# Seven-product feed-forward of a two-layer decoder trunk: the last product of each group moved behind the first of the next, and the matmuls of a product ordered bank by bank

## The chip, the cores and the metric

The kernel runs on one core of one Trainium2 chip. The metric is the device time of one execution in microseconds (us). The engines are called by their short names: PE is the matrix engine (PEld its weight loads), DVE the vector engine, ACT the scalar engine, POOL the general one, and SP the queue that issues nearly all DMA transfers. PSUM is the memory of 8 banks into which PE accumulates; SBUF holds everything else.

## The reference, cut to what matters

Two layers; each is a half-step SwiGLU feed-forward, a mixing block of three attentions, and a second half-step SwiGLU, with RMSNorm around each. Only the feed-forwards are touched:

```python
def _swiglu(t, w_gate, w_up, w_down):
    return (jax.nn.silu(t @ w_gate) * (t @ w_up)) @ w_down
...
for l in range(DEPTH):                                   # 2
    f = _swiglu(_rmsnorm(h, ffn1_pre_g[l]), ffn1_w_gate[l], ffn1_w_up[l], ffn1_w_down[l])
    h = h + 0.5 * _rmsnorm(f, ffn1_post_g[l])
    ...                                                  # the mixing block
    f = _swiglu(_rmsnorm(h, ffn2_pre_g[l]), ffn2_w_gate[l], ffn2_w_up[l], ffn2_w_down[l])
    h = h + 0.5 * _rmsnorm(f, ffn2_post_g[l])
```

There are 512 tokens, the model width is 1024 and the hidden width 2816. Everything is float32.

## The kernel before, in words

**Precision.** A float32 operand is split into a high and a low part, and each tile product is three matmuls into the same PSUM bank (`mm3`): high by high (line 205), high by low (206), low by high (207). Weights arrive as `raw_...` tiles by DMA. ACT casts a raw tile to its high part `wh_...` (line 182), DVE then subtracts to get the low part `wl_...` (line 183). There are four buffers for `wh` and four for `wl`.

**Groups of seven products.** The first 2048 hidden columns stand in two chunks of 1024 (`ci` 0 and 1). For each chunk the gate matrix product (a *group* called G) and the up matrix product (U) are done with seven half-size products in place of eight (`token_product`), in the order 0, 2, 1, 3, 4, 5, 6 of `ORDER`. So there are four groups in a feed-forward, G0, U0, G1, U1. Each product has two units of weights (two contraction tiles of 128 in each, 512 columns) and two token tiles (`e` 0 and 1), hence 2 x 2 x 2 x 3 = 24 matmuls of 128x512. It uses two PSUM banks, one for each `e`. Three pairs of banks serve a group: product 0 opens pair 0 (tag `z`), product 2 pair 2 and product 1 pair 1 (tag `mm`). Products 3, 5 and 6 accumulate again into pair 0, and 4 into pair 2. After each product but 0 the banks are read by ACT (line 775 copies, line 786 the SiLU) or DVE (lines 777 and 779 add or multiply). Products 5 and 6 stand next to each other and write the same pair of banks. Some units need a difference of two weight blocks first; DVE makes it (line 327).

**Down part.** The down projection of these 2048 columns is 14 such products (`product`, kind `d`), seven for each chunk; between them stand plain products of the last 768 columns (`ga_18` and so on). A first factor comes from the hidden rows `hr`, split by `first_factor` into `ah` and `al`. Results of an up group are turned with DMA transposes on SP (`turn`, lines 800, 801, 804).

**Order.** `PLAN` lists the jobs of a feed-forward, each one product. When a job begins, the weights of the next jobs, four units, are loaded (`load_ahead`), in the order of the jobs. The program order is then changed by a scheduler of the framework, which may put a later instruction ahead of one that it expects to wait; each engine then runs its instructions strictly in the resulting order. A kernel is one chain of jobs: two layers with two feed-forwards each, so four times through `PLAN`.

**Names.** In the program's order a bank is `pwa0u_0_1`: feed-forward `a0` (first of layer 0; `c0` is the second; `a1`, `c1` in layer 1), `u` for up or `g` for gate, then chunk or pair and `e`. The weights are `wh_ua_0_5_2`: up weights, chunk 0, product 5, unit at contraction tile 2. `pda` and `pdc` are banks of the down products, `wh_da_0_0_0` is down, chunk 0, product 0. Numbers after that count buffers. The profile leaves out these numbers, so that U0 and U1 of one feed-forward are both `pwa0u`.

Of the kernel before, what the change touches and what calls it, by code (L numbers as in the profile page):

```python
# [18 lines left out]
P = 128  # L19
# [4 lines left out]
def kernel(  # L24
# [38 lines left out]
    nc = tc.nc  # L63
    _, S, D = x.shape
# [34 lines left out]
    def tmp(name):  # L99
        return sb.tile([P, S], F32, tag="f32t", bufs=5, name=name)  # L100
# [3 lines left out]
    def stile(shape, tag, name, dt=F32R):  # L104
        return sb.tile(shape, dt, tag=tag, bufs=BUFS[tag], name=name)
# [4 lines left out]
    def pbank(tag, name):  # L110
        return ps.tile([P, S], F32, tag=tag, bufs=4, name=name)
# [91 lines left out]
    def mm3(pt, lh, ll, rh, rl, start, stop, free=False):  # L203

        nc.tensor.matmul(pt, lh, rh, start=start, stop=False, skip_group_check=free)  # L205
        nc.tensor.matmul(pt, lh, rl, start=False, stop=False, skip_group_check=free)  # L206
        nc.tensor.matmul(pt, ll, rh, start=False, stop=stop, skip_group_check=free)  # L207
# [391 lines left out]
    SUM = (0, 1, 2, 0, 2, 0, 0)  # L599
# [3 lines left out]
    def ffn(l, src, wg, wu, wd, dst, name, spare, parked, plan, aside=None):  # L603
# [6 lines left out]
        hid, st = {}, {}  # L610
# [5 lines left out]
        def hidden_rows(i):  # L616
            if i not in hr:
                hr[i] = stile([P, FC // 2, S], ("k", "tri")[i // 2], f"hr{name}_{i}", F32)
            return hr[i]
# [114 lines left out]
        def in_product(n):  # L734
            if n in (0, 1, 6):
                i, j = ((0, 0), (0, 1), None, None, None, None, (1, 1))[n]
                return [block(i, j, part) for part in range(2)]
            return st["u", n]

        def token_product(ci, up, n, uns):  # L740

            nm = f"{name}{'gu'[up]}_{ci}_{n}"
            if n in (0, 1, 2):
                st["c", n] = [pbank("z" if n == 0 else "mm", f"pw{nm}_{e}") for e in range(2)]
            if n == 1:
                for e in range(2):
                    nc.scalar.copy(st["c", 1][e][:], st["c", 0][e][:])
            if n == 0:
                if not up:
                    st["s", ci] = {}  # L750
            pts = st["c", SUM[n]]
            h, l = in_product(n)
            opens, ends = n in (0, 2), n in (1, 4, 6)
            for un in uns:
                for k in range(un.nk):
                    kk = un.k0 + k
                    for e in range(2):
                        c = slice(e * P, (e + 1) * P)
                        mm3(pts[e][:], h[:, kk, c], l[:, kk, c], un.h[:, k], un.l[:, k], opens and kk == 0,
                            ends and kk == ND // 2 - 1, free=True)  # L760
                        yield 3 * S * PE_US
                    turn(kk)
            if n == 0:
                return
            q = TO[n]
            g = st["s", ci]
            if not up and q not in g:
                g[q] = stile([P, FC // 2, S // 2], "f", f"s{name}_{ci}_{q[0]}{q[1]}", F32)[:]
            g = g[q]
            r = hidden_rows(2 * ci + q[1])[:, :, HALVES[q[0]]] if up else g  # L770
            for e in range(2):
                p = pts[e][:].rearrange("p (f q) -> p f q", f=2)
                re, ge = r[:, 2 * e:2 * e + 2], g[:, 2 * e:2 * e + 2]
                if n in (2, 3):
                    nc.scalar.copy(re, p)
                elif n in (4, 5):
                    nc.vector.tensor_tensor(re, re, p, ALU.add)
                elif up:
                    nc.vector.tensor_tensor(ge, p, ge, ALU.mult)
                else:  # L780
                    nc.scalar.activation(re, p, AF.Silu)
            if n in (4, 5):
                if up:
                    nc.vector.tensor_tensor(g, r, g, ALU.mult)
                else:
                    nc.scalar.activation(r, r, AF.Silu)
            if up and n in (1, 4, 5, 6):
                turns.append([nm, g, (2 * ci + q[1], q[0]), n in (1, 5), 0, None])

        def turn(kk):  # L790

            for one in turns:
                nm, g, (row, i), own, age, planes = one
                if kk == 1 and age == 0:
                    one[5] = planes = ([stile([P, 2, 2 * S], "rs", "tr" + nm, U16)[:, h] for h in range(2)] if own else
                                       [tmp(f"tr{nm}_{h}")[:].bitcast(U16) for h in range(2)])
                    words = g.rearrange("p f q -> p (f q)").bitcast(U16)
                    for h, plane in enumerate(planes):
                        part = tmp(f"th{nm}_{h}")[:].bitcast(U16)
                        nc.scalar.copy(part, words[:, h::2])  # L800
                        nc.sync.dma_start_transpose(plane.rearrange("p (r q) -> p r q", q=P), part)
                if kk in (0, 1) and age == 2:
                    r = hidden_rows(row)[:].bitcast(U16)
                    nc.scalar.copy(r[:, :, i * S + kk:(i + 1) * S:2].rearrange("p f (e q) -> p e f q", e=2),
                                   planes[kk].rearrange("p (e f q) -> p e f q", e=2, q=P))
                if kk == ND // 2 - 1:
                    one[4] += 1
            turns[:] = [one for one in turns if one[4] < 3]
# [42 lines left out]
        def product(at, uns):  # L851
            ci, n = DOWN[at]
            first, last = ci == 0, ci == NC - 1
            if at == 0:
                RINGS["o"] = 2
                dst.begin()
            if at + 1 < len(DOWN):
                first_factor(*DOWN[at + 1])
            if first and n in (0, 2):
                st["b", SUM[n]] = [pbank("z", f"pd{name}_{n}_{e}") for e in range(2)]  # L860
            pts = st["b", SUM[n]]
            h, l = st.pop(("a", ci, n))
            opens, ends = first and n in (0, 2), last and n in (1, 4, 6)
            for un in uns:
                for k in range(un.nk):
                    kk = un.k0 + k
                    for e in range(2):
                        c = slice(e * P, (e + 1) * P)
                        mm3(pts[e][:], h[:, kk, c], l[:, kk, c], un.h[:, k], un.l[:, k], opens and kk == 0,
                            ends and kk == FC // 2 - 1, free=True)  # L870
                        yield 3 * S * PE_US
                    turn(kk)
            if not last:
                return
            if n == 0:
                st["b", 1] = [pbank("z", f"pd{name}_1_{e}") for e in range(2)]
                for e in range(2):
                    nc.scalar.copy(st["b", 1][e][:], pts[e][:])
                return
            i, hf = TO[n]  # L880
            for e in range(2):
                f = dst.fs[2 * i + e][:, HF[hf]]
                if n in (4, 5):
                    nc.vector.tensor_tensor(f, f, pts[e][:], ALU.add)
                else:
                    nc.scalar.copy(f, pts[e][:])
# [753 lines left out]
            sub.turned(t)  # L1640
            yield ("pe", 0.9)

    PLAN = 7 * [("G", 0)] + [("m", 0)] + 7 * [("U", 0)] + 7 * [("G", 1)] + 6 * [("U", 1)] + [("a", 0), ("U", 1)]
    downs = iter(14 * [("d", 0)])
    slots = iter([(kind, f, m) for f in (18, 20) for kind in "gu" for m in range(2)])
    for n in (2, 2, 1, 1, 2, 2, 1, 1):
        PLAN += list(itertools.islice(downs, n)) + [next(slots)]
    PLAN += list(downs)

# [8 lines left out]
    for l in LAYERS:  # L1658
        i, mn = 3 * l, []
        ma = ffn(l, subs[i], ffn1_w_gate, ffn1_w_up, ffn1_w_down, subs[i + 1], f"a{l}", "v",  # L1660
                 park[2 * l] if l else None, PLAN, lambda l=l, mn=mn: mem_norm(l, mn))
        rest = mem_kv(l, mn, *kvs[l])
# [11 lines left out]
        mb["run"]()  # L1674
        mc = ffn(l, subs[i + 2], ffn2_w_gate, ffn2_w_up, ffn2_w_down, subs[i + 3], f"c{l}", "o", park[2 * l + 1], PLAN)
        for part, units in zip(mb["next"], (mc["early"][:2], mc["early"][2:])):
# [27 lines left out]
```

## Time and profile before

| | |
|---|---|
| Time, median of 3 runs | 2383.74 us (2383.66 to 2387.1) |
| The profiled execution's own time | 2382.98 us |
| Its span, first to last instruction | 2380.9 us (2.08 us lie around it) |
| PE busy | 2350.6 us, 99% of the span, 11719 matmuls |
| PEld busy | 1984.2 us, 83% |
| DVE busy | 1803.5 us, 76% |
| ACT busy | 1513.8 us, 64% |
| Granted PE clock, mean | 0.998 |
| DMA | 354.98 MB, 149 GB/s |

A matmul of the profile is shown from its start to its modelled end, 0.39 us for the 128x512 ones; the next one starts 0.23 us after it in a dense stream, so these rows overlap. What a wait costs is therefore read from start to start. In the views, `L183` is line 183 of the kernel, `pda<-wl_da,aha` is the written tile and the read ones, and a bracket at a row's end is idle time of the engine before the row with what ended it.

### The profile page before, as it was taken

The numbers are of one execution on the slowest core, as the hardware profiler recorded it, in microseconds if no ns is written. First come the engines' busy times: TensorE is split into PE (matmuls) and PEld (weight loads), VectorE is DVE, ScalarE is ACT, GpSimd is POOL, SyncE is SP. The second block draws the span as 40 slices with busy tenths as digits, with TensorE's granted clock in tenths as the row PEclk, the third lists the DMA queues.
The fourth block names the chain that finished last, engine by engine and source line by source line (L and its number), as shares of the span: only waits on it lengthen the run. The fifth ranks groups of instructions, "written<-read, shape, count | busy, mean of one in ns | idle before, by whom it ended". The sixth has DMA issues, their size and how long they took to land.

```text
span 2380.9 us, 31151 instructions
## 1 busy us (share of the span) xinstructions
PE 2350.6 (99%) x11719; PEld 1984.2 (83%) x11719; DVE 1803.5 (76%) x2358; ACT 1513.8 (64%) x2306; POOL 75.8 (3%) x134
## 2 busy tenths in 40 slices
PE   9999999999999999999999999999999999999998
PEld 7787889888888888778888878889888888888787
DVE  8886877667777689778788778766767767888785
ACT  6777465577766556775656665655777665567744
POOL 0000000000111000000000000000001100000000
PEclk9999999999999999999999999999999999999999
DMA  5666455223223556664647664542323235566643
GB/s 197 195 174 174 161 196 151 71 80 94 87 78 103 189 179 182 170 195 135 236 128 200 186 185 153 192 124 71 94 76 98 73 123 193 161 204 174 197 143 141
DMA packets 299754, 354.98 MB, mean 149 GB/s; under 512 B 78266, under 2 KB 192978, under 8 KB 299604
## 3 DMA queue, kind: packets, MB, share of 16 engines
q1 hardware_dynamic: 299508, 352.97, 48.0%
q8 instruction: 92, 1.51, 0.3%
q14 instruction: 58, 0.48, 0.1%
q0 software_dynamic: 96, 0.03, 0.0%
HBM read 319.39 MB, written 16.78 MB: 141 GB/s over the span
## 4 chain that ended last, share of the span: by engine, by line
PE 85%; DVE 5%; DMA 4%; ACT 4%; issue 2%; SPq 0%; DVEq 0%; ACTq 0%
PE pg L206 4%; PE pg L205 4%; PE pg L207 4%; PE pdc L206 3%; PE pdc L207 3%; PE pdc L205 3%; PE pda L206 2%; PE pda L207 2%; PE pda L205 2%; PE pb L207 2%; PE pb L206 2%; PE pb L205 2%; PE pq L206 1%; PE pq L205 1%; PE pk L207 1%
## 5 line engine op out<-in xcount | busy, mean ns | idle before, releaser
L205 PE MATMUL pg<-us_a,wh_wg 128*128 128x512 f32 x384 | 151.0, 393 | 0.0
L207 PE MATMUL pg<-us_a,wl_wg 128*128 128x512 f32 x384 | 149.8, 390 | 0.0
L206 PE MATMUL pg<-us_a,wh_wg 128*128 128x512 f32 x384 | 149.8, 390 | 0.0
L206 PE MATMUL pdc<-wl_dc,ahc 128*128 128x512 f32 x224 | 87.9, 392 | 3.6 <-DVE wl_dc L183 3.6
L206 PE MATMUL pda<-wl_da,aha 128*128 128x512 f32 x224 | 87.9, 392 | 3.6 <-DVE wl_da L183 3.6
L205 PE MATMUL pda<-wh_da,aha 128*128 128x512 f32 x224 | 86.8, 390 | 2.0 <-ACT wh_da L182 2.0
L205 PE MATMUL pdc<-wh_dc,ahc 128*128 128x512 f32 x224 | 86.8, 390 | 0.6 <-ACT wh_dc L182 0.6
L207 PE MATMUL pda<-wh_da,ala 128*128 128x512 f32 x224 | 87.3, 390 | 0.0
L207 PE MATMUL pdc<-wh_dc,alc 128*128 128x512 f32 x224 | 87.2, 389 | 0.0
L183 DVE TENSOR_TENSOR wl_da<-raw_da,wh_da 128x1024 fp32r<-128x1024 f32 x50 | 60.9, 1224 | 34.3 <-ACT wh_da L182 34.3
L207 PEld LDWEIGHTS pg<-us_a,wl_wg 128*128 128x128 f32 x384 | 72.1, 188 | 15.2
L206 PEld LDWEIGHTS pg<-us_a,wh_wg 128*128 128x128 f32 x384 | 72.2, 188 | 14.1
L205 PEld LDWEIGHTS pg<-us_a,wh_wg 128*128 128x128 f32 x384 | 72.1, 188 | 14.1
L183 DVE TENSOR_TENSOR wl_dc<-raw_dc,wh_dc 128x1024 fp32r<-128x1024 f32 x50 | 61.0, 1223 | 29.0 <-ACT wh_dc L182 28.9
L182 ACT CAST wh_da<-raw_da 128x1024 fp32r<-128x1024 f32 x50 | 52.2, 1050 | 45.6 <-PE pda L207 15.3
L182 ACT CAST wh_dc<-raw_dc 128x1024 fp32r<-128x1024 f32 x50 | 52.3, 1049 | 42.7 <-PE pdc L207 18.0
L186 DVE SCALAR_TENSOR_TENSOR wl_wg<-raw_wg,wh_wg 128x1024 fp32r<-128x1024 f32 x48 | 58.4, 1221 | 22.3 <-ACT wh_wg L185 22.3
L200 DVE SCALAR_TENSOR_TENSOR ga<-pg,bgate,ga 128x512 f32<-128x512 f32 x48 | 35.9, 747 | 50.5 <-ACT ga L199 50.5
L185 ACT ACTIVATE wh_wg<-raw_wg 128x1024 fp32r<-128x1024 f32 x48 | 50.5, 1057 | 24.6 <-PE pv L1096 11.7
L183 DVE TENSOR_TENSOR wl_uc<-raw_uc,wh_uc 128x1024 fp32r<-128x1024 f32 x44 | 53.7, 1220 | 16.2 <-ACT wh_uc L182 16.2
L183 DVE TENSOR_TENSOR wl_ua<-raw_ua,wh_ua 128x1024 fp32r<-128x1024 f32 x44 | 53.6, 1220 | 16.0 <-ACT wh_ua L182 16.0
L182 ACT CAST wh_uc<-raw_uc 128x1024 fp32r<-128x1024 f32 x44 | 46.1, 1050 | 30.4 <-PE pgc L206 7.6
(647 smaller groups left out, 8057.6 us busy)
## 6 DMA issues: line engine op xcount, KB each, us to landing
raw_da<-in_ffn_w_down_dram SPq DMA_DIRECT2D x66, 512.0 KB, 4.5
raw_dc<-in_ffn_w_down_dram SPq DMA_DIRECT2D x66, 512.0 KB, 3.9
raw_ga<-in_ffn_w_gate_dram SPq DMA_DIRECT2D x52, 512.0 KB, 4.2
raw_ua<-in_ffn_w_up_dram SPq DMA_DIRECT2D x52, 512.0 KB, 4.5
raw_gc<-in_ffn_w_gate_dram SPq DMA_DIRECT2D x52, 512.0 KB, 3.9
raw_uc<-in_ffn_w_up_dram SPq DMA_DIRECT2D x52, 512.0 KB, 3.6
raw_wg<-in_w_gate_dram SPq DMA_DIRECT2D x48, 512.0 KB, 3.6
raw_wo<-in_w_out_dram SPq DMA_DIRECT2D x24, 512.0 KB, 3.3
```

The lines of the kernel that those rows point to most:

```text
L182: both = [nc.scalar.copy(h_ap, src)]
L183: make = lambda: nc.vector.tensor_tensor(l_ap, src, h_ap.bitcast(F32), ALU.subtract)
L185: both = [nc.scalar.activation(h_ap, src, AF.Copy, scale=scale)]
L186: make = lambda: nc.vector.scalar_tensor_tensor(l_ap, src, scale, h_ap.bitcast(F32), ALU.mult, ALU.subtract)
L200: nc.vector.scalar_tensor_tensor(t, z, minus, t, ALU.max, ALU.add)
L205: nc.tensor.matmul(pt, lh, rh, start=start, stop=False, skip_group_check=free)
L206: nc.tensor.matmul(pt, lh, rl, start=False, stop=False, skip_group_check=free)
L207: nc.tensor.matmul(pt, ll, rh, start=False, stop=stop, skip_group_check=free)
```

## The change

Two edits, and a renaming that they need (the bank pairs are now kept per group, since two groups are open at once).

```diff
             for un in uns:
-                for k in range(un.nk):
-                    kk = un.k0 + k
-                    for e in range(2):
-                        c = slice(e * P, (e + 1) * P)
+                for e in range(2):
+                    c = slice(e * P, (e + 1) * P)
+                    for k in range(un.nk):
+                        kk = un.k0 + k
                         mm3(pts[e][:], h[:, kk, c], l[:, kk, c], un.h[:, k], un.l[:, k], opens and kk == 0,
                             ends and kk == ND // 2 - 1, free=True)
                         yield 3 * S * PE_US
-                    turn(kk)
+                    turn(un.k0 + e)
...
-    PLAN = 7 * [("G", 0)] + [("m", 0)] + 7 * [("U", 0)] + 7 * [("G", 1)] + 6 * [("U", 1)] + [("a", 0), ("U", 1)]
-    downs = iter(14 * [("d", 0)])
+    PLAN = 6 * [("G", 0)] + [("U", 0), ("G", 0), ("m", 0)] + 5 * [("U", 0)] + [("G", 1), ("U", 0)] + 5 * [("G", 1)]
+    PLAN += [("U", 1), ("G", 1)] + 5 * [("U", 1)] + [("a", 0), ("d", 0), ("U", 1), ("d", 0)]
+    downs = iter(12 * [("d", 0)])
     slots = iter([(kind, f, m) for f in (18, 20) for kind in "gu" for m in range(2)])
-    for n in (2, 2, 1, 1, 2, 2, 1, 1):
+    for n in (0, 2, 1, 1, 2, 2, 1, 1):
```

The loop edit is made in `token_product` and, word for word the same, in `product`. Within one unit the matmuls went bank 0, bank 1, bank 0, bank 1, three at a time; now six go into bank 0 and six into bank 1. The `PLAN` edit exchanges, at each of the four borders G0 to U0, U0 to G1, G1 to U1 and U1 to the down products, product 6 of the old group with product 0 of the new one. The number and shapes of the matmuls stay.

On PE at the border from U0 to G1 of the first feed-forward, before: `ga_1_0` is the first product of G1, `ua_0_6` the last of U0.

```order
L207 MATMUL pwa0u_0_1_829<-wh_ua_0_5_2_948,ula_5_665 128x512
L205 MATMUL pwa0g_0_0_1134<-wh_ga_1_0_0_1029,us_x_130 128x512
L206 MATMUL pwa0g_0_0_1134<-wl_ga_1_0_0_1030,us_x_130 128x512
L207 MATMUL pwa0g_0_0_1134<-wh_ga_1_0_0_1029,us_x_130 128x512
L205 MATMUL pwa0g_0_1_1135<-wh_ga_1_0_0_1029,us_x_130 128x512
L205 MATMUL pwa0u_0_0_828<-wh_ua_0_6_0_987,us_x_131 128x512
L206 MATMUL pwa0u_0_0_828<-wl_ua_0_6_0_988,us_x_131 128x512
L207 MATMUL pwa0u_0_0_828<-wh_ua_0_6_0_987,us_x_131 128x512
L205 MATMUL pwa0u_0_1_829<-wh_ua_0_6_0_987,us_x_131 128x512
```

And now, at the same place:

```order
L207 MATMUL pwa0u_0_1_782<-wh_ua_0_5_2_948,ula_5_665 128x512
L205 MATMUL pwa0g_0_0_1088<-wh_ga_1_0_0_986,us_x_130 128x512
L206 MATMUL pwa0g_0_0_1088<-wl_ga_1_0_0_987,us_x_130 128x512
L207 MATMUL pwa0g_0_0_1088<-wh_ga_1_0_0_986,us_x_130 128x512
L205 MATMUL pwa0g_0_0_1088<-wh_ga_1_0_0_986,us_x_130 128x512
L206 MATMUL pwa0g_0_0_1088<-wl_ga_1_0_0_987,us_x_130 128x512
L207 MATMUL pwa0g_0_0_1088<-wh_ga_1_0_0_986,us_x_130 128x512
L205 MATMUL pwa0g_0_1_1089<-wh_ga_1_0_0_986,us_x_130 128x512
```

Before, the scheduler had already put four matmuls of the new group ahead of the old group's last product; now all 24 stand there, and the six-and-six order shows.

On ACT at the border from U1 to the down products, before: the casts of the weights, with the copies of line 804 and 800 (the turning of results) between them.

```order
L182 CAST wh_ua_1_5_2_1544<-raw_ua_1_5_2_1389 128x1024
L775 COPY hra_3_1492<-pwa0u_0_1_1431 128x2x256
L182 CAST wh_ua_1_6_0_1583<-tua_1_0_1261 128x1024
L804 COPY hra_2_1531<-tra0u_1_1561 128x2x4x128
L182 CAST wh_ua_1_6_2_1588<-tua_1_2_1263 128x1024
L182 CAST aha_1_0_1738<-hra_2_1531 128x1024
L800 COPY tha0u_4_0_1649<-sa_1_01_1296 128x1024
L182 CAST wh_da_0_0_0_1623<-raw_da_0_0_0_1539 128x1024
```

And now:

```order
L182 CAST wh_ua_1_5_2_1544<-raw_ua_1_5_2_1389 128x1024
L775 COPY hra_3_1492<-pwa0u_0_1_1392 128x2x256
L182 CAST wh_da_0_0_0_1582<-raw_da_0_0_0_1425 128x1024
L804 COPY hra_2_1533<-tra0u_1_1561 128x2x4x128
L182 CAST wh_da_0_0_2_1590<-raw_da_0_0_2_1427 128x1024
L182 CAST aha_1_0_1688<-hra_2_1533 128x1024
L182 CAST wh_ua_1_6_0_1622<-tua_1_0_1259 128x1024
L800 COPY tha0u_4_0_1649<-sa_1_01_1296 128x1024
```

The cast of the first down weights moves from behind both casts of `ua_1_6` and three copies to the place directly behind the bank copies of line 775; the casts of `ua_1_6` follow it.

More of the change, by code (lines that the diff above doesn't have):

```diff
@@ L743, in token_product @@
             if n in (0, 1, 2):
-                st["c", n] = [pbank("z" if n == 0 else "mm", f"pw{nm}_{e}") for e in range(2)]
+                st["c", ci, up, n] = [pbank("z" if n == 0 else "mm", f"pw{nm}_{e}") for e in range(2)]
             if n == 1:
                 for e in range(2):
-                    nc.scalar.copy(st["c", 1][e][:], st["c", 0][e][:])
+                    nc.scalar.copy(st["c", ci, up, 1][e][:], st["c", ci, up, 0][e][:])
             if n == 0:
@@ L750, in token_product @@
                     st["s", ci] = {}
-            pts = st["c", SUM[n]]
+            pts = st["c", ci, up, SUM[n]]
             h, l = in_product(n)
@@ L864, in product @@
             for un in uns:
[L865 to L868, printed above, removed]
+                for e in range(2):
+                    c = slice(e * P, (e + 1) * P)
+                    for k in range(un.nk):
+                        kk = un.k0 + k
                         mm3(pts[e][:], h[:, kk, c], l[:, kk, c], un.h[:, k], un.l[:, k], opens and kk == 0,
@@ L871, in product @@
                         yield 3 * S * PE_US
-                    turn(kk)
+                    turn(un.k0 + e)
             if not last:
```

## The prediction

> **What bounds the kernel now.** The page comes first: one engine is busy all the time, and the others are not.
>
> ```profile
> span 2380.9 us, 31151 instructions
> PE 2350.6 (99%) x11719; PEld 1984.2 (83%) x11719; DVE 1803.5 (76%) x2358; ACT 1513.8 (64%) x2306; POOL 75.8 (3%) x134
> ```
>
> The matmuls are the same before and after in number and shape, so the change can only win back what PE loses between them, and can only cost what it adds there. The second view is that of waits, for PE alone, longest first. The rows that I use:
>
> ```profile
> PE pdc L206 <- DVE wl_dc L183: 3.6, 4, 1.3
> PE pda L206 <- DVE wl_da L183: 3.6, 4, 1.3
> PE pda L205 <- ACT wh_da L182: 2.0, 2, 1.6
> PE pwa0g L205 <- ACT wh_ga L182: 1.4, 1, 1.4
> ...
> PE pwa1g L206 <- DVE wl_ga L183: 0.8, 1, 0.8
> PE pwa1u L206 <- DVE wl_ua L183: 0.8, 1, 0.8
> PE pwc0u L206 <- DVE wl_uc L183: 0.8, 1, 0.8
> PE pwc0g L206 <- DVE wl_gc L183: 0.8, 1, 0.8
> PE pwc1g L206 <- DVE wl_gc L183: 0.8, 1, 0.8
> PE pwa0g L206 <- DVE wl_ga L183: 0.8, 1, 0.8
> PE pwc1u L206 <- DVE wl_uc L183: 0.7, 1, 0.7
> ...
> PE pdc L205 <- ACT wh_dc L182: 0.6, 2, 0.4
> ...
> PE pwc0u L205 <- ACT wh_uc L182: 0.6, 1, 0.6
> ```
>
> Columns: who waits for whom, us in all, times, the longest. Nearly all of PE's idle time is for weights, first the high part, then the low part, once or twice in a group. The third view, the timeline of PE at the border from U0 to G1 of the first feed-forward, shows where. Columns: start, duration, operation.
>
> ```profile
> 111.69 0.39 PE L207 MATMUL pwa0u<-wh_ua,ula 128*128 128x512 f32 x1
> 113.51 0.50 PE L205 MATMUL pwa0g<-wh_ga,us_x 128*128 128x512 f32 x1 [1.44 <-ACT wh_ga L182]
> 114.77 0.50 PE L206 MATMUL pwa0g<-wl_ga,us_x 128*128 128x512 f32 x1 [0.76 <-DVE wl_ga L183]
> 115.11 0.40 PE L207 MATMUL pwa0g<-wh_ga,us_x 128*128 128x512 f32 x1
> 115.34 0.39 PE L205 MATMUL pwa0g<-wh_ga,us_x 128*128 128x512 f32 x1
> 115.57 0.58 PE L205 MATMUL pwa0u<-wh_ua,us_x 128*128 128x512 f32 x1
> ...
> 119.22 0.40 PE L205 MATMUL pwa0u<-wh_ua,us_x 128*128 128x512 f32 x1
> ```
>
> The dense spacing is 0.23 us (115.11 to 115.34 to 115.57). The four matmuls of `pwa0g` are those that the scheduler put ahead of U0's last product. Their weights were loaded as those of the job *behind* that product, and they come just too late. So the stall is one of order: the early matmuls ask for weights one product too soon.
>
> **The change part by part: the exchange at the borders.** The job order now says what PE does, so product 0 of the new group gets its weights ahead of product 6 of the old. What is that worth? Two products at the border from U1 to the down part, on DVE and PE, show an early product against an ordinary one:
>
> ```profile
> 194.40 1.23 DVE L183 TENSOR_TENSOR wl_da<-raw_da,wh_da 128x1024 fp32r<-128x1024 f32 x1
> 200.75 1.23 DVE L183 TENSOR_TENSOR wl_da<-raw_da,wh_da 128x1024 fp32r<-128x1024 f32 x1 [0.52 <-ACT wh_da L182]
> 195.69 0.50 PE L206 MATMUL pda<-wl_da,aha 128*128 128x512 f32 x1 [0.76 <-DVE wl_da L183]
> 206.74 0.39 PE L206 MATMUL pda<-wl_da,aha 128*128 128x512 f32 x1
> ```
>
> The early one has its low part at 195.63 and PE takes it at 195.69. The next down product, in its place by the list, has it at 201.98 and needs it at 206.74: 4.76 us of cover. I expect the moved products to have cover like that, and the waits to go.
>
> Now the price of a wait, start to start, from the border rows above. A wait for a high part costs its idle time and 0.15 (111.69 to 113.51 is 1.82, less 0.23 for a dense step is 1.59, against 1.44). A wait for a low part costs idle + 0.27 (1.26 less 0.23 is 1.03, against 0.76), and the matmul behind it another 0.11 (0.34 instead of 0.23).
>
> High parts at the borders: 2.0 + 1.4 + 0.6 + 0.6 = 4.6 us in six waits, with 6 x 0.15 that is 5.5.
>
> Low parts: of the four `pda` and the four `pdc` waits some do not lie at a border. The waits of PE in 215:330 and in 1050:1192 only, past the border, in the two feed-forwards of layer 0:
>
> ```profile
> PE pda L206 <- DVE wl_da L183: 1.3, 1, 1.3
> PE pdc L206 <- DVE wl_dc L183: 1.3, 1, 1.3
> ```
>
> These are fourth down products, whose weights are late for another reason, as I read the kernel: the plain product before them keeps two of the four weight buffers. I take it that layer 1 has one of 0.8 in each feed-forward too, since 3.6 less 1.3 is three of 0.77. These four stay. At the borders are then four of 0.77 (3.1) and the seven single rows (5.5): 8.6 us in eleven waits, with 11 x 0.38 that is 12.8.
>
> Twice PE's granted clock falls behind such a wait; rows of the windows view, the clock third from the end:
>
> ```profile
> 111.50:120.00 8.50, 6.31 (x20) 4.47 (x19) 5.76 (x6) 6.05 (x6) 0.00 (x0) 0.80 0.93 242
> 995.50:1000.00 4.50, 4.41 (x13) 3.33 (x13) 1.96 (x3) 1.06 (x1) 0.00 (x0) 0.62 0.81 240
> ```
>
> 0.20 of 8.5 and 0.38 of 4.5 are 1.7 each; from 115.57 to 119.22 nine matmuls take 3.65 instead of 2.04, 1.6. Together 3.3, which goes with the waits.
>
> *The rule beside it.* The Trainium skill, "TensorE: Matmul & The Clock Gate", Part 1, says that the clock halves after about 3.4 us idle in a free-running window. Here 1.44 and 0.76 us of idle within 3.3 us sufficed, so the trace does not bear that length out as an unbroken gap. By the rule alone these two spells would not belong to the waits and could stay, and the sum below would be 3.3 us less.
>
> At three borders PE also goes back from one or two early matmuls to the old group. At the third border of `c0`:
>
> ```profile
> 995.18 0.50 PE L206 MATMUL pwc0u<-wl_uc,us_b 128*128 128x512 f32 x1 [0.76 <-DVE wl_uc L183]
> 995.78 0.50 PE L205 MATMUL pwc0g<-wh_gc,us_b 128*128 128x512 f32 x1
> ```
>
> 0.60 instead of 0.23, that is 0.37, of which 0.11 is counted already: 3 x 0.26 is 0.8.
>
> The exchange therefore takes away 5.5 + 12.8 + 3.3 + 0.8 = 22.4 us.
>
> **What it moves.** The old group's banks for product 6 now get a whole product (24 x 0.227 = 5.4 us) to be read out after product 5, where they had five matmuls or fewer. The new group opens another pair of banks. The old pair is held one product longer; it is next wanted by the group after. A raw tile of product 0, which product 2 uses again, is held over one more product; that is the one resource in which the new order asks for more. Its transfers also move on SP: those for product 6 now stand behind those for the next group's product 0, and a difference on DVE (line 327) waits for them with later splits queued behind it. I cost this at nothing, by the cover of 4.76 us above; the first rival is what happens without.
>
> The schedule has one early plain matmul more per feed-forward, inside the fourth down product. The same thing stands in the trace before, at another down product:
>
> ```profile
> 282.02 0.39 PE L205 MATMUL pga<-us_x,wh_ga 128*128 128x512 f32 x1
> 282.35 0.50 PE L206 MATMUL pda<-wl_da,aha 128*128 128x512 f32 x1
> ```
>
> 0.33 in place of 0.23, and the matmul behind a broken step cost another 0.11 above: 0.2 each, 0.8 in all.
>
> **Six and six.** Does it cost to stay in a bank, or to change it? The plain products put 24 matmuls in a row into one bank, the border rows change after three:
>
> ```profile
> L205 PE MATMUL pg<-us_a,wh_wg 128*128 128x512 f32 x384 | 151.0, 393 | 0.0
> ```
>
> 393 ns against 0.39 us: no price to either. What it does is to finish bank 0 six matmuls before the product's end instead of three, 3 x 0.227 = 0.7 us sooner for its reader, and to need bank 1 later by as much. No wait of the list above is for a bank, so this is worth nothing now; between 0 and, if it eased all four remaining 0.3 to 1.3 us waits, 4 us of gain.
>
> **Sum.** 22.4 less 0.8 is 21.6 us. On the profiled execution: 2382.98 - 21.6 = 2361.4. That execution lies 0.8 under the median of the runs, so 2362.1 against 2383.74. What is late next are the four waits at the fourth down product, some 5 us in all, which I leave in.
>
> **Rivals.**
> *It turns slower: the waits move behind the moved product.* Place: SP and DVE at each border. The transfer for product 6 is issued late, DVE waits in line 327, and splits for the running product stand behind it. For it: SP does wait long for raw tiles to come free.
>
> ```profile
> SPq L297 <- DVE wl_ua L183: 88.2, 33, 9.9
> ```
>
> Against it: 88.2 over 33 is 2.7 us, under the 4.76 of cover, and only the longest, 9.9, is over it. A wait of 9.9 would leave 9.9 - 4.76 = 5.1 us on PE; it decides from 21.6 / 16 = 1.4 us on PE at each of the 16 borders. At half that excess on each, 2.6 us, the change is 16 x 2.6 - 21.6 = 20 us slower: about 2404.
>
> *Half of it returns.* DVE, the busiest engine behind PE, or ACT, held by the transposes, are late for some borders: waits at eight of 16 borders, 11 us gained: about 2373. For it: the cover is 4.76 us only where I looked.
>
> *Nothing to see.* The scheduler already had new matmuls at the border; the exchange makes explicit what it did, and the waits only fall on the first matmuls of a product that is now early. Then within 4.8 us of 2383.7. Against it: in the order on ACT the cast for the first down product moves ahead of both casts of product 6.
>
> *The clock spells stay* as by the page's rule: 21.6 - 3.3 = 18.3, about 2365; inside my range.
>
> **How the numbers follow.** About 0.2%, 4.8 us, is what a measurement of this kernel can tell from no change. The forecast, waits gone with or without the clock spells, gets 0.78 (of it 0.08 for the spells that stay); half returned 0.10; nothing to see 0.05; slower 0.07. The forecast and the half are faster: 0.88; same 0.05; slower 0.07. The range goes from the forecast with the bank gain of 4 us and 2 us of small resumptions that I did not count, 2356, to the half that returns, 2373; it leaves out the last two cases and a little of each end.
>
> **What would show it.** In the profile after: no PE wait for `wh` or `wl` on `pwa..`/`pwc..` tiles; `pda` and `pdc` waits of one each per feed-forward instead of two or three; the clock of the two windows near 1.00; PE's busy time little changed with the span some 21 us shorter. Wrong, if waits of PE on `wl_u..` or on a bank's readers (lines 775, 777, 779) stand at the borders, or if `L327` waits for DMA have grown.

## The result, and the profile after

The changed kernel takes 2413.46 us (median of 4 runs, 2411.98 to 2415.68), against 2384.02 us (2383.66 to 2387.1) for the kernel before beside it: the ratio is 1.0123, 95% interval 1.0102 to 1.0144. It is 29 us slower; the forecast was 22 us faster (2356 to 2373). The profiled execution took 2415.68 us; the head of its page:

```profile
span 2413.9 us, 31143 instructions
PE 2357.9 (98%) x11719; PEld 1993.7 (83%) x11719; DVE 1800.6 (75%) x2358; ACT 1515.8 (63%) x2305; POOL 75.5 (3%) x134
```

The same 11719 matmuls; the span is 33.0 us longer, and PE is busy 7.3 us longer, which fits the slower matmuls shown below. The view of waits, PE alone, longest first (us in all, times, longest):

```profile
PE pda L206 <- DVE wl_da L183: 7.5, 2, 3.9
PE pdc L206 <- DVE wl_dc L183: 7.4, 2, 5.0
PE pwc1g L205 <- ACT pwc1g L747: 7.2, 1, 7.2
PE pwa1g L205 <- ACT pwa1g L747: 6.1, 1, 6.1
PE pwa0g L205 <- ACT pwa0g L747: 5.8, 1, 5.8
PE pwc0g L205 <- ACT pwc0g L747: 5.1, 1, 5.1
...
PE pdc L205 <- ACT pdc L878: 1.2, 2, 0.8
```

The weight waits at the borders are gone, as forecast. Two other kinds of wait have come, each once in each of the four feed-forwards: four for line 747, the copy of pair 0 into pair 1 onto which product 1 is added, and four for a low part of a down product. A smaller third kind is for line 878, the same copy of banks in the down part. The timeline of PE in the first feed-forward (start, duration, operation; a bracket is idle time before it) shows the border from U0 to G1, G1's step from product 2 to product 1, and the fourth down product:

```profile
111.46 0.39 PE L207 MATMUL pwa0u<-wh_ua,ula 128*128 128x512 f32 x1
111.68 0.39 PE L205 MATMUL pwa0g<-wh_ga,us_x 128*128 128x512 f32 x1
111.91 0.39 PE L206 MATMUL pwa0g<-wl_ga,us_x 128*128 128x512 f32 x1
...
127.78 0.39 PE L207 MATMUL pwa0g<-wh_ga,ula 128*128 128x512 f32 x1
134.01 0.80 PE L205 MATMUL pwa0g<-wh_ga,us_x 128*128 128x512 f32 x1 [5.85 <-ACT pwa0g L747]
...
138.44 0.47 PE L206 MATMUL pwa0g<-wl_ga,us_x 128*128 128x512 f32 x1
...
223.40 0.39 PE L205 MATMUL pda<-wh_da,aha 128*128 128x512 f32 x1
227.69 0.79 PE L206 MATMUL pda<-wl_da,aha 128*128 128x512 f32 x1 [3.90 <-DVE wl_da L183]
```

At the border, where 1.44 and 0.76 us of idle stood before, the new group follows at the dense step, 0.22 to 0.23 us. Sixteen microseconds later PE stands for 5.85 us, and then the next ten matmuls take 4.43 us (134.01 to 138.44) instead of 2.27. PE's granted clock in 127 to 140 us is 0.74 here, and was 1.00 before.

**The whole loss in one count.** For each matmul of 512 columns I take the time from its start to the next start, less the dense step of 0.2266 us, and sum it by product. Over the whole program this excess is 47.6 us in the trace before and 81.0 in the trace after: 33.4 more, against 33.0 of span. With some 8600 such matmuls, a step larger by 0.0002 us takes 1.7 us off every kernel's sum alike, so the differences are firmer than the sums. Its parts:

| | before | after |
|---|---|---|
| the 16 borders | 23.9 | none over 0.15 a product |
| G1, step from product 2 to product 1 (four times) | 0 | 34.8 |
| fourth down product (four times) | 5.4 | 22.5 |
| step from the first plain gate product to the third down product (waits for L878) | 0 | 2.3 |
| all else | 18.3 | 21.4 |

**The copy in G1.** ACT in the trace after, in the time in which PE stands (127.8 to 134.0):

```profile
127.45 1.04 ACT L800 COPY tha0u<-sa 128x1024 uint16<-128x1024 uint16 x1
128.39 1.05 ACT L182 CAST wh_ga<-tga 128x1024 fp32r<-128x1024 f32 x1
129.34 1.05 ACT L800 COPY tha0u<-sa 128x1024 uint16<-128x1024 uint16 x1
130.28 0.58 ACT L775 COPY sa<-pwa0g 128x512 f32<-128x512 f32 x1
130.76 1.33 ACT L804 COPY hra<-tra0u 128x1024 uint16<-128x1024 uint16 x1
131.95 1.04 ACT L182 CAST wh_ga<-tga 128x1024 fp32r<-128x1024 f32 x1
132.89 0.58 ACT L775 COPY sa<-pwa0g 128x512 f32<-128x512 f32 x1
133.37 1.07 ACT L747 COPY pwa0g<-pwa0g 128x512 f32<-128x512 f32 x2
```

ACT never idles here. Pair 0 is ready for the copy since product 0 of G1 ended (24 matmuls from 111.68, about 117.1), but the copy stands behind six microseconds of work that PE does not wait for, among it the two L800 that turn the result of U0's product 6. That product now comes behind the whole of G1's product 0, so its two copies run at 127.45 and 129.34. Before, they ran at 124.15 and 126.05, ahead of these rows of ACT:

```profile
128.22 1.04 ACT L182 CAST wh_ga<-raw_ga 128x1024 fp32r<-128x1024 f32 x1
129.17 1.06 ACT L747 COPY pwa0g<-pwa0g 128x512 f32<-128x512 f32 x2
...
133.55 0.57 ACT L775 COPY sa<-pwa0g 128x512 f32<-128x512 f32 x1
```

Here the copy stands ahead of line 775, and is done by 130.23; PE begins product 1 at 132.64 and waits for nothing.

**The fourth down product.** DVE in the trace after:

```profile
217.32 1.22 DVE L183 TENSOR_TENSOR wl_da<-raw_da,wh_da 128x1024 fp32r<-128x1024 f32 x1 [0.27 <-ACT wh_da L182]
222.53 1.23 DVE L327 TENSOR_TENSOR bta<-bta,raw_da 128x1024 f32<-128x1024 f32 x1 [3.99 <-DMA raw_da<-in_ffn_w_down_dram]
225.28 1.22 DVE L327 TENSOR_TENSOR bta<-bta,raw_da 128x1024 f32<-128x1024 f32 x1 [1.52 <-DMA raw_da<-in_ffn_w_down_dram]
226.42 1.22 DVE L183 TENSOR_TENSOR wl_da<-raw_da,wh_da 128x1024 fp32r<-128x1024 f32 x1
```

The last row is the low part that PE waits for. DVE stands ahead of it in two differences of line 327 for the product *after* it, and these wait for raw tiles. On SP, those tiles are issued behind the transposes of U1's moved product 6:

```profile
210.88 3.08 SPq L801 DMA_TRANSPOSE tra0u<-tha0u  x2
...
214.91 1.23 SPq L801 DMA_TRANSPOSE tra0u<-tha0u  x1
216.25 0.56 SPq L297 DMA_DIRECT2D raw_da<-in_ffn_w_down_dram  x1
...
217.43 0.47 SPq L297 DMA_DIRECT2D raw_da<-in_ffn_w_down_dram  x1
```

### The profile page after: what moved, and what is told of

Same layout as the page of the kernel before. It is cut to its first block, busy times and chain, and to the rows that moved or that the text cites. A ratio compares the mean times of both kernels' runs of the same rounds, so it can differ in the third digit from the quotient of the medians.

```text
span 2413.9 us, 31143 instructions
## 1 busy us (share of the span) xinstructions
PE 2357.9 (98%) x11719; PEld 1993.7 (83%) x11719; DVE 1800.6 (75%) x2358; ACT 1515.8 (63%) x2305; POOL 75.5 (3%) x134
## 4 chain that ended last, share of the span: by engine, by line
PE 87%; DMA 4%; DVE 4%; ACT 3%; issue 2%; SPq 0%; POOL 0%; DVEq 0%; ACTq 0%
PE pg L207 4%; PE pg L206 4%; PE pg L205 4%; PE pda L206 3%; PE pda L207 3%; PE pda L205 3%; PE pdc L206 3%; PE pdc L207 2%; PE pdc L205 2%; PE pb L205 2%; PE pb L207 2%; PE pb L206 2%; PE pq L206 1%; PE pq L205 1%; PE pq L207 1%
## 5 line engine op out<-in xcount | busy, mean ns | idle before, releaser
L207 PEld LDWEIGHTS pg<-us_a,wl_wg 128*128 128x128 f32 x384 | 72.1, 188 | 15.2
L183 DVE TENSOR_TENSOR wl_gc<-raw_gc,wh_gc 128x1024 fp32r<-128x1024 f32 x40 | 48.6, 1219 | 26.5 <-ACT wh_gc L182 26.3
L183 DVE TENSOR_TENSOR wl_ga<-raw_ga,wh_ga 128x1024 fp32r<-128x1024 f32 x40 | 48.5, 1219 | 26.3 <-ACT wh_ga L182 26.2
L182 ACT CAST wh_ua<-raw_ua 128x1024 fp32r<-128x1024 f32 x44 | 46.2, 1052 | 34.6 <-PE pwa1g L207 10.1
```

Source lines behind the costliest of these rows:

```text
L182: both = [nc.scalar.copy(h_ap, src)]
L183: make = lambda: nc.vector.tensor_tensor(l_ap, src, h_ap.bitcast(F32), ALU.subtract)
```

## The experiments

**Theory A**: the time is lost in two queues, ACT's in G1 and DVE's at the fourth down product, because an instruction that PE waits for stands behind others that it does not. **Rivals**: the exchange holds the bank pairs too long, however the queues stand (B); six-and-six is bad by itself (C); at the down part SP is simply too late (D). The first two rows below are those of the result; the other kernels were measured in three groups, each beside the kernel before, whose median was 2384.82, 2385.88 and 2380.3 us there. Across groups the ratios compare, not the microseconds. The excess is the count above, from each kernel's profiled execution.

| kernel | us | ratio to before (95%) | excess |
|---|---|---|---|
| before | 2384.0 | 1 | 47.6 |
| changed | 2413.5 | 1.0123 (1.0102 to 1.0144) | 81.0 |
| list alone | 2384.2 | 0.9995 (0.9986 to 1.0004) | 48.1 |
| six-and-six alone | 2384.4 | 0.9998 (0.9985 to 1.0012) | 50.5 |
| changed, early copy | 2381.1 | 0.9977 (0.9968 to 0.9986) | 44.2 |
| changed, early copy, L327 held | 2359.8 | 0.9894 (0.9879 to 0.9909) | 25.2 |
| changed, border U1 to down taken back | 2405.7 | 1.0081 (1.0063 to 1.0100) | 72.1 |
| changed, border U0 to G1 taken back | 2388.6 | 1.0003 (0.9990 to 1.0017) | 54.4 |
| list alone, L327 held | 2368.0 | 0.9921 (0.9903 to 0.9939) | 29.6 |
| before, early copy, L327 held | 2400.6 | 1.0058 (1.0043 to 1.0074) | 64.1 |
| changed, L327 held | 2392.0 | 1.0041 (1.0026 to 1.0056) | 57.8 |
| before, L327 held | 2374.9 | 0.9975 (0.9962 to 0.9988) | 38.7 |
| list, early copy, L327 held, old loops | 2363.6 | 0.9921 (0.9906 to 0.9936) | 27.9 |

The profiled span less the excess lies between 2332 and 2334 us for every row, before and after included. So what changes the time is all in the steps between these matmuls.

### Each edit alone

The list alone is the changed kernel with the old loops; the renaming stays:

```diff
-                for e in range(2):
-                    c = slice(e * P, (e + 1) * P)
-                    for k in range(un.nk):
-                        kk = un.k0 + k
+                for k in range(un.nk):
+                    kk = un.k0 + k
+                    for e in range(2):
+                        c = slice(e * P, (e + 1) * P)
...
-                    turn(un.k0 + e)
+                    turn(kk)
```

> The new list of jobs with the old loops (three matmuls into one bank, three into the other). Theory A: the time is lost because ACT's two copies of line 747 in G1 stand behind the two bank copies of line 775, and at the fourth down product because DVE stands in line 327 with splits behind it. The first needs both edits: with the old loops the copies of line 747 stand ahead of line 775 again in ACT's order. So A expects PE's waits for L747 gone, about 35 us less than the changed kernel, with the waits for wl_d at the fourth down product left: about 2378 us (2373 to 2384). Rival B: the exchange itself holds the banks too long, however ACT is ordered: 2411 to 2416. Rival C: six-and-six is bad by itself, everywhere: then all of the loss goes and the border gain of 24 us stays, about 2362.

Six-and-six alone is the changed kernel with the `PLAN` lines of before.

> Six-and-six alone, with the list of jobs of before. Theory A: nothing is displaced on ACT or DVE, and staying in a bank costs or gains nothing: 2384 us, within 3. Rival C (six-and-six is bad by itself): 2400 to 2415, with PE waits for line 747 or for banks.

Both came out at the time of before: 0.9995 and 0.9998. Neither edit alone changes the time; together they cost 29 us. For the list this is a balance, not nothing: the border waits are gone, and the fourth down product loses about as much. That rules out C, and B in the plain form that the exchange alone is enough. The list alone, PE's waits:

```profile
PE pda L206 <- DVE wl_da L183: 7.3, 2, 3.7
PE pdc L206 <- DVE wl_dc L183: 6.6, 2, 4.1
PE pwa0u L205 <- ACT pwa0u L747: 2.5, 2, 2.0
...
PE pwc1g L205 <- ACT pwc1g L747: 1.2, 1, 1.2
```

The fourth down product loses 22.5 us here too, but of the long L747 waits in G1 only one of 1.2 and one of 0.4 us are left. ACT's order in G1 has the copy ahead again:

```profile
130.30 1.06 ACT L747 COPY pwa0g<-pwa0g 128x512 f32<-128x512 f32 x2
...
135.75 1.04 ACT L800 COPY tha0u<-sa 128x1024 uint16<-128x1024 uint16 x1
136.70 1.07 ACT L775 COPY sa<-pwa0g 128x512 f32<-128x512 f32 x2
```

So the late place of the copy needs both edits. A reason that fits, argued and not shown: with six-and-six, bank 0 of product 2 is finished six matmuls before its end, its L775 copy counts as ready earlier, and the scheduler, which takes ready work in the program's order, puts it ahead of the copy of line 747, which is written later. The 2384.2 us are 6 over the 2378 that I expected, partly for the L747 waits in U0 (2.5 us), which I had not counted.

### The copy's place, moved two ways

The copy is written one product earlier, at the start of product 2:

```diff
-            if n in (0, 1, 2):
+            if n in (0, 2):
                 st["c", ci, up, n] = [pbank(...) for e in range(2)]
-            if n == 1:
+            if n == 2:
+                st["c", ci, up, 1] = [pbank("mm", f"pw{nm[:-1]}1_{e}") for e in range(2)]
                 for e in range(2):
                     nc.scalar.copy(st["c", ci, up, 1][e][:], st["c", ci, up, 0][e][:])
```

> The changed kernel, with the copy of line 747 moved in the program from the start of product 1 to the start of product 2, one product earlier, so that it stands ahead of line 775 on ACT. Theory A: PE's four waits for L747 in G1 (7.2, 6.1, 5.8 and 5.1 us, some 35 us with the half-clock stretches behind them) go and nothing else changes: about 2378 us (2373 to 2385). Rival B: the copy waits for the banks and not for its place, so PE waits as before: 2411 to 2416. If the cause is ACT's load as such, half comes back as waits for wh: about 2396.

2381.1 us, ratio 0.9977 against 1.0123: some 35 us less than the changed kernel. The long waits for the copy are gone; what is left of that kind in the list of PE's waits is one of 0.4 us, behind the untouched down waits:

```profile
PE pdc L206 <- DVE wl_dc L183: 8.5, 2, 4.7
PE pda L206 <- DVE wl_da L183: 6.4, 2, 3.9
...
PE pwa0g L205 <- ACT pwa0g L748: 0.4, 1, 0.4
```

(Line 748 is line 747 here.) ACT runs the two copies of the first G1 far ahead of PE's need for them, which comes at 126.97 us:

```profile
115.32 0.58 ACT L748 COPY pwa0g<-pwa0g 128x512 f32<-128x512 f32 x1
...
124.65 0.62 ACT L748 COPY pwa0g<-pwa0g 128x512 f32<-128x512 f32 x1
```

So the banks of pair 1 were free by then, with all four borders exchanged. The other way is to leave the copy and take back the exchange from U0 to G1, by which the turning of U0's product 6 had come into G1:

```diff
-    PLAN = 6 * [("G", 0)] + [("U", 0), ("G", 0), ("m", 0)] + 5 * [("U", 0)] + [("G", 1), ("U", 0)] + 5 * [("G", 1)]
+    PLAN = 6 * [("G", 0)] + [("U", 0), ("G", 0), ("m", 0)] + 6 * [("U", 0)] + 6 * [("G", 1)]
```

> The changed kernel with the exchange at the border from U0 to G1 taken back alone. Theory A: U0's product 6 ends one product sooner, its transposing copies are off ACT before G1's product 2, and the copies of line 747 stand ahead of line 775 again: the 35 us there go, and the border's waits for weights come back (about 8 us): about 2387 us (2382 to 2392). Rival (the bank pairs of both groups held over the other three exchanges): the L747 waits stay, 2413 + 8, about 2420.

2388.6 us, ratio 1.0003, with no L747 wait in G1: about 29 us less than the changed kernel. The 34.8 us of the copy go here too, and some 9 us of waits at this border come back. So the loss goes whether the copy is moved away from the work or the work from the copy. That is what A says, and B falls: three borders are still exchanged in this kernel, and four with the early copy.

### The fourth down product

The exchange from U1 to the down products is taken back:

```diff
-... [("a", 0), ("d", 0), ("U", 1), ("d", 0)]
+... [("a", 0), ("U", 1), ("d", 0), ("d", 0)]
```

> The changed kernel with the exchange at the border from U1 to the down products taken back; the other three borders stay exchanged. Theory A says that the fourth down product is late because that exchange puts U1's last transposes on SP ahead of the raw tiles that line 327 needs. Then its excess of 22.5 us goes back to the 5.4 of before, the small waits for line 878 (2.3 us) go, and the border's own waits come back (some 8 us over the four feed-forwards); the four waits for L747 in G1 stay. 2413 - 17 - 2 + 8 is about 2402 us (2397 to 2406). Rival: the fourth down product is late because everything ahead of it was moved, not this border: 2413 + 8, about 2420.

2405.7 us, at the upper end of A's range. The four fourth down products lose 9.5 us, where the changed kernel lost 22.5; three are back at 0.7 to 1.5, one (in `c0`) still has a wait of 3.0 and loses 6.0; why it keeps that is open. So this border brought most of it, but not every one of the four times.

Then the place on DVE alone: line 327 for product 0_2 is held behind all that is written ahead of it.

```diff
-                if Q.pinned:
+                if Q.pinned or self.name[0] == "d" and "_0_2_" in self.name:
                     tc.keep_in_program_order(ins)
```

> The changed kernel with only the second mend: line 327 for down product 0_2 held behind the splits of product 1_1 on DVE, the copy of line 747 left in its late place. If the two losses are independent, the fourth down product's excess of 22.5 us goes to some 4 and the 35 us at L747 stay: about 2396 us (2391 to 2401). If removing one only uncovers the other, more than 2405.

2392.0 us: 1.0041 against 1.0123, about 20 us less. The excess at the four products is 3.4 us, that at L747 stays (33.4). The two losses are independent. With SP's order unchanged the wait is gone, so D falls: the tiles were late only for the splits that stood behind line 327.

> The kernel before with the second mend alone (line 327 behind the splits), old list, old loops, old place of the copy. The run with both mends and no exchange came out at 2400.6 us, 15 slower than before. If the early copy is what cost there (it stands in G1 behind a full ACT, at 973 us in that trace), this one is not slower but gains the 5.4 us of the fourth down product, less some 2: about 2380 us (2376 to 2384). If holding line 327 is what cost, about 2400.

The kernel before with this edit alone: 0.9975, 6 us faster than before. The waits that I had "left in" as no part of the change were the same fault, and this is a gain that has nothing to do with the change.

### Both mended

The early copy and the held line 327 in the changed kernel:

> As the run with the early copy, and the two differences of line 327 for down product 0_2 are held behind the splits of down product 1_1 on DVE. Theory A with its second part (DVE's place in line is what PE waits for at the fourth down product): 22 us of excess there go back to some 5 or less, so 17 us less than the run with the early copy: about 2362 us (2357 to 2370). Rival: SP issues the raw tiles too late behind the transposes, and the wait only moves to the next product: as the run with the early copy, about 2378, or in between.

2359.8 us, ratio 0.9894: 25 us faster than the kernel before, the best of all that were run. PE's waits, and DVE at the place shown above:

```profile
PE pda L206 <- DVE wl_da L183: 1.2, 2, 0.6
...
PE pdc L206 <- DVE wl_dc L183: 0.6, 1, 0.6
```

```profile
213.73 1.22 DVE L183 TENSOR_TENSOR wl_da<-raw_da,wh_da 128x1024 fp32r<-128x1024 f32 x1 [4.57 <-ACT wh_da L182]
...
217.15 1.22 DVE L183 TENSOR_TENSOR wl_da<-raw_da,wh_da 128x1024 fp32r<-128x1024 f32 x1
218.28 1.22 DVE L327 TENSOR_TENSOR bta<-bta,raw_da 128x1024 f32<-128x1024 f32 x1
```

Line 327 now stands behind both splits and waits for nothing.

> The new list of jobs with the old loops, and line 327 for down product 0_2 held behind the splits of product 1_1 on DVE. From the run of the list alone (2384.2 us), the excess at the fourth down product (6.6, 6.1, 5.5 and 4.4 us, 22.5 in all) should shrink to about 1 each: about 2366 us (2361 to 2371). Against the 2359.8 us of the kernel with both edits and both mends, what is left (waits for L747 in several groups, 2.5 + 1.2 us, and the steps behind them) shows what the early copy is worth here. Rival: SP's late raw tiles bind, and less than half is won: over 2375.

The list with the held line 327 and the old loops, 2368.0 us: as expected. Adding the early copy to that:

> The new list of jobs with both mends and the old loops: against the kernel with both mends and six-and-six (2359.8 us) it shows what six-and-six is worth, and against the new list with the second mend alone (2368.0) what the early copy is worth with the old loops. If the loop order is worth nothing once the copy stands early: 2360 us (2356 to 2365). If six-and-six is what gives the copy its room: 2366 or more.

0.9921, the same as without the early copy. With the old loops the early copy is worth nothing, since the copy was not late. What six-and-six is worth in the mended kernel is not settled: 0.9894 (0.9879 to 0.9909) with it and 0.9921 (0.9906 to 0.9936) without, from different groups, with intervals that just overlap; the excess differs by 2.7 us.

### The mends without the change

> The kernel before with the two mends and neither edit of the change: the early copy of line 747 and line 327 held behind the splits. If the 24.9 us that the mended change won are the exchange's own, this wins only what the fourth down product loses before, 5.4 less some 3: 2379 to 2384 us. If the mends by themselves bring it and the exchange nothing, about 2360.

A miss: 2400.6 us, 15 slower than before, outside both expectations. Since holding line 327 alone gains 6 us in this kernel, the early copy costs here. The trace says how; ACT in `c0`:

```profile
971.46 1.04 ACT L182 CAST wh_gc<-raw_gc 128x1024 fp32r<-128x1024 f32 x1
972.41 1.04 ACT L801 COPY thc0u<-sc 128x1024 uint16<-128x1024 uint16 x1
973.36 0.58 ACT L748 COPY pwc0g<-pwc0g 128x512 f32<-128x512 f32 x1
```

PE stood 2.02 us for this copy (its rows are in the last section). Steps of this kind in the four G1 come to 10.7 us, where the excess is 25.4 above that of the kernel before with line 327 held alone. The rest lies in waits at the borders and in other places; what the early copy has to do with these was not traced, and the kernel before with the early copy alone was not run. The mend moves the copy's place in the program, not its place in the queue. In this list it again lands behind a full ACT, so it is a mend for one list and no rule.

## Why the prediction was wrong

**The borders: right.** 22.4 us were to go. The count finds 23.9 at the borders before and none there after, and with both new waits mended the kernel is 25 us faster than before. Six of these come from line 327 held, so the change with the early copy brings some 19.

**"What it moves", costed at nothing: this step failed.** The price was read from a cover of 4.76 us between a low part and its use. That cover is one for weights, at one place. The moved product carries two other things: its turning on ACT (line 800, with line 804 behind the transpose) and its transposes on SP. The text named SP and line 327, let the same cover hide them, and gave ACT's copies no term; a rival names ACT only as "held by the transposes". The chain that broke in G1 is one of banks, pair 0 copied to pair 1, two products past the border, where I had not compared ACT's order. Term by term: 34.8 us at L747, 17.1 more at the fourth down product and 2.3 at L878, where nothing stood.

**The four waits "left in" at some 5 us** became 22.5. I explained them by two weight buffers held by the plain product. The run with line 327 held brings the excess there in the kernel before from 5.4 to 0.6 us with the same buffers, so that explanation was wrong: the cause was DVE's order.

**Six and six, "worth nothing".** Alone that is what it is (0.9998). The 393 ns read for it are a duration with a modelled end and could not show a step; the runs do, since the span less the excess is the same with both loops. But the term was added to the others as if the two edits were independent. They are not: the loss in G1 comes only with both.

**The slower rival** named half of what came: line 327 waiting for tiles late on SP, with splits behind. It put the price at 2.6 us for each of 16 borders; it came at four places, all past the fourth border, 4.3 us more each. By itself that would have left a small gain or nothing, as the list alone shows (2384.2 us). The larger half, the copy in G1, was none of my rivals. The sign to look for, grown L327 waits for DMA, was named rightly.

**The clock.** The two spells at the borders went with their waits, so the rival in which they stay did not come; but the longer waits brought longer spells, 2.2 us behind the first of the rows above.

## What to carry to other kernels

When a job is moved in a list, price everything that hangs on its end, on each engine and for some products past the border: the copies, transposes and bank handovers that follow it, not only the weights ahead of it. Two edits that each leave the time as it was can meet in a scheduler, so read the instruction order of both together, and look on each in-order engine for an instruction that PE waits for behind ones that it does not. Where such a wait stands already, a mend of one line can be worth trying first; holding line 327 gave 6 us to the kernel before.

## What the runs showed of the hardware

A wait of PE can cost more than itself, by the clock behind it. After 5.85 us of idle the next ten matmuls started 0.44 us apart on average instead of 0.227, 2.2 us more. In the kernel with the mends alone, 2.02 us of idle were enough for a spell of at least 2.7 us (973.99 to 976.71, six matmuls in place of the 1.36 us they take in a dense stream):

```profile
973.99 0.80 PE L205 MATMUL pwc0g<-wh_gc,us_b 128*128 128x512 f32 x1 [2.02 <-ACT pwc0g L748]
974.58 0.63 PE L205 MATMUL pwc0g<-wh_gc,uhc 128*128 128x512 f32 x1
975.01 0.63 PE L206 MATMUL pwc0g<-wl_gc,uhc 128*128 128x512 f32 x1
...
976.71 0.63 PE L207 MATMUL pwc0g<-wh_gc,ulc 128*128 128x512 f32 x1
```

The steps behind the first are 0.43 us, and the granted clock from 973.99 to 977.20 us is 0.50. Size alone does not decide: 1.97 us of idle in the list alone (at 91.42 us) and 2.51 us in the kernel with the border U0 to G1 taken back (at 2249.15 us) have no such spell behind them, with steps of 0.23 to 0.34 us. The Trainium skill, "TensorE: Matmul & The Clock Gate", Part 1, gives at least one idle window of about 3.4 us before the clock falls; the spell after 5.85 us agrees with that, the one after 2.02 us does not.
